# One-hot rows of a token's picks: four wide f16 operations with a step of four, or twelve narrow ones with per-partition scalars, side by side

## The chip, the cores and the metric

The kernel runs on 1 core of one Trainium2 chip. The metric is the device time of one execution in microseconds (us).

## The reference, cut to what matters

The program is two transformer blocks on 256 tokens of 1024 columns. The last part of the second block is a mixture of 16384 small experts ("PEER"): each of 8 heads picks 16 experts per token by two half keys, and the gates are a softmax over the 16 scores.

```python
best_s, pos = lax.top_k(cand_s, PEER_TOPK)
idx = jnp.take_along_axis(cand_i, pos, axis=-1)   # idx = i * 128 + j
g = jax.nn.softmax(best_s, axis=-1)
u = expert_u[idx]
act = jax.nn.gelu(jnp.einsum('cd,chkd->chk', xb, u).astype(jnp.float32), approximate=False)
w = (g * act).astype(xb.dtype)
return jnp.einsum('chk,chkd->cd', w, expert_v[idx])
```

A token has 8 x 16 = 128 picks, each a pair (i, j) with a gate g.

## The kernel before, in words

The kernel gathers no expert. It multiplies all 16384 rows of u with all tokens, in 128 blocks (i) of 128 rows (j), and weighs the result W[j, i, t] = gelu(u x) with a dense gate G[j, i, t] that is zero where token t did not pick (i, j). Then it multiplies W with all rows of v.

`peer` (L1261) holds this. Its main loop runs over 144 blocks of weights of 128x1024: 16 of the query weights, then 128 of u. For each block the program writes, in this order:

- `fetch` (L118), which loads a block three ahead by SP's queue, rounds it to float32r on ScalarE (`hi`, L114) and leaves the rest on VectorE (`lo`, L115); hi and lo have four buffers each;
- what is in the list `pend`: the spread of a group of gates into W, and the product of W with the gates that are known already (L1512);
- `proj_tile` (L352), 24 matmuls of 128x256 (L143 to L145) that need hi and lo of the block;
- what is in the list `late`: products of gates;
- gelu on ScalarE (L1508 into W for the tokens whose gates come later, L1511 into `act` for those whose gates are there);
- `work(PACE)` (L1429), which sets the order of the work around the change. VectorE's side work is a generator: the top-k of 8 heads, the lists of picks, then `gates` for eight tokens at a time, 32 times. Each piece yields the microseconds that it is booked at, and with every block pieces are taken until 1.4 of these are used up. VectorE's instructions stay in the order in which the program writes them.

`gates(n0)` (L1440) makes G for eight tokens. IT, JT, GH and GL hold, with the pick on the partition and the token on the column, the indices i and j and the gate in two f16 parts. For one token, G[j, i] = sum over the picks of onehot(j) onehot(i) g: a matmul over the 128 picks with bj (the one-hot of j) as weights and ah and al (the one-hot of i times the two parts) as moving operands. The rows of 128 are compared with `io4`, the numbers 0 to 127, each four times. Four operations on VectorE make them for eight tokens at once, with the four tokens of a group innermost, so that a token's row is read with a step of four elements:

```python
nc.vector.tensor_tensor(bj, hot, bc(JT), op=OP.is_equal)
nc.vector.tensor_tensor(ah, hot, bc(IT), op=OP.is_equal)
yield 1.2 * PGT
nc.vector.tensor_tensor(al, ah, bc(GL), op=OP.mult)
nc.vector.tensor_tensor(ah, ah, bc(GH), op=OP.mult)
```

`product` (L1455) issues eight matmuls for four tokens (L1459, L1460); `spread` (L1463) multiplies the result into W for the blocks that are done (VectorE, L1469) and copies it into W for those to come (ScalarE, L1471). ah, al and bj have two buffers each.

Of the kernel before, what the change touches and what calls it, by code (L numbers as in the profile page):

```python
# [12 lines left out]
F16 = mybir.dt.float16  # L13
# [4 lines left out]
OP = mybir.AluOpType  # L18
AX = mybir.AxisListType
DRAM = bass.MemoryType.DRAM  # L20
# [21 lines left out]
NTK, NLS, NGT = 11, 11, 3  # L42
# [33 lines left out]
class Body:  # L76
# [25 lines left out]
    # blocks of weights in the order of their use, each loaded and split exactly into two float32r parts  # L102
    def plan(self, *specs):
        """specs (name, index, width)"""
        self.todo.extend(specs)
# [12 lines left out]
    def fetch(self, n=None, low=None):  # L118
        """units loaded until the number ahead, or n more"""
        n = self.ahead - len(self.loaded) if n is None else n  # L120
        while self.todo and n > 0:
            spec = self.todo.popleft()
            self.loaded.append((spec[:2], self.load(*spec, low or (self.nc.gpsimd if spec[:2] in POOLED else self.nc.vector))))
            n -= 1
# [10 lines left out]
    def warm(self, n, p=None):  # L135
        """products of no use that keep TensorE's clock up through a wait"""
# [10 lines left out]
    def rstd(self, ss, n, width, beside=None):  # L147
        """1/sqrt(ss/width + eps) for ss [p, n]; beside: work in the wait for the square root"""
# [7 lines left out]
    def rstd_steps(self, ss, n, width):  # L156
        """the same as a list of steps"""
# [7 lines left out]
        # a step of Newton's on the table's value  # L165
# [9 lines left out]
    def setup(self):  # L175
# [3 lines left out]
        # the table of square roots, before its first use  # L179
# [3 lines left out]
        # rows of L1 columns, and 16 more behind the last  # L183
# [7 lines left out]
        # rows of tokens and the gate of the last sum; they wait in DRAM while the experts need their room  # L191
# [11 lines left out]
    # ---------------------------------------------------------------- the first block  # L203
    def ada_units(self, parts, acc, room):
        """silu(c) * w_ada of the parts named, summed over blocks of rows into acc; a block of 128 x 1024 each time"""
# [16 lines left out]
    def ada_cols(self, n0, s, later=None):  # L222
        """shift or scale s of the six (sh_a sc_a g_a sh_f sc_f g_f) as columns; later: takes what is left to be called"""
# [17 lines left out]
    def ada_row(self, s, dst, acc, ones, later=None):  # L241
        """gate s of the six on all partitions, from its sums acc"""
# [14 lines left out]
    def start(self, pool):  # L257
        """hn^T split; the meta rows between the two tiles of tokens"""
        nc, t = self.nc, self.t
        # in rooms that later tiles take  # L260
# [14 lines left out]
        def norm(tt):  # L275
            """1 / rms of a tile of rows, its halves squared beside each other"""
# [12 lines left out]
        def scaled(x, n, r, banks, w):  # L289
            """the transposes of x's rows, each times its r"""  # L290
# [49 lines left out]
    def proj(self, out, wh, wl, apart):  # L340
        """W^T x for a tile of columns; apart: the products with x's second part after the others"""
# [10 lines left out]
    def proj_tile(self, name, i=None, m=128, n=T, real=False):  # L352
        """W^T x for one tile of columns: bank [m, n] of the first n tokens, or without the meta rows between them"""
# [13 lines left out]
    def t5_bias(self, w):  # L367
        """per head [128 queries, keys]: keys of the block before, meta (for tile 1), of the block, meta (for tile 0)"""
# [13 lines left out]
        # a step back for each partition: from copies of the vectors, as many partitions at a time as there are copies  # L382
# [11 lines left out]
    # softmax of a pair of heads over two tiles of queries, then P V; the columns of a unit u = 2*tile + head  # L394
    def attend(self, outs, oc, qT, kT, bias, nk, sink, exp_scale, v, vmeta, gain, meta):
        """qT(tile, head), kT(head, n) give operands; bias(tile, head) an addend or None;
        nk the keys of each tile (the meta rows at 128, if meta); v(chunk, head) [128, 64]"""
# [7 lines left out]
        for tl in range(2):  # L405
            n, o = nk[tl], tl * nk[0]
            for hd in range(2):
                # the two heads' products run beside each other, each into its own bank
# [40 lines left out]
        # transposes of P: chunks of 128 keys  # L449
# [50 lines left out]
    def steps(self, gens, fills):  # L500
        """pairs of heads through the stages of attend, each stage a step after the one before; fills: work of TensorE
        beside them in each step"""
# [10 lines left out]
    def part(self, acc, items, tt, hf):  # L513
        """acc[tt][hf] += o[:, tt]^T w for items (o, w, start, stop)"""
# [4 lines left out]
    def out_proj(self, acc, items):  # L519
        """acc[tt][half] += o[:, tt]^T w for items (o, w, start, stop)"""  # L520
# [10 lines left out]
    def scaled_add(self, tt, hf, acc, r, row, add=None):  # L531
        """a half of h[:, tt] += acc * r * row"""
# [6 lines left out]
    def transposed4(self, src, hf):  # L539
        """bank with the transposes of four blocks of src's columns"""  # L540
# [8 lines left out]
    def pre(self, acc, t1, lnrow, ss, tt, hf, gain=True):  # L549
        """what the norm of acc takes from a finished half; gain: False for the squares alone, None for the gain alone"""  # L550
# [16 lines left out]
    def gained(self, p, y, c0, h, l, by, later=None):  # L567
        """a bank of transposes into operands, with gains from column c0 on; by: the engine of the second parts, which
        are put off into later"""
# [7 lines left out]
    def scaled(self, xn, r, tt, hf):  # L577
        """a half of h / rms(h), transposed"""
# [4 lines left out]
    def shifted(self, y, p, tt, hf, n0, by="act", steps=False):  # L583
        """a bank of transposes times 1 + scale and plus shift; or the steps of it"""
# [21 lines left out]
    def roots(self, x):  # L606
        """the table of square roots, once x is there"""
# [7 lines left out]
    def first_block(self):  # L615
# [21 lines left out]
        # forget gates: log sigmoid, then the sums over positions  # L637
# [6 lines left out]
        # c / (1 + exp(-c))  # L644
# [42 lines left out]
        def values(p, dst, c, dstm, zi):  # L687
            vT = A.tile([128, L1], F32, name=self.nm("vT"), tag="vT", bufs=2)
            nc.scalar.activation(vT, p, AF.Copy)
            # meta rows, one head to 16 partitions and its own columns  # L690
# [102 lines left out]
        # the last products and the step to the next operands; the gain goes on here, the rows' norm on the products  # L793
# [18 lines left out]
        with self.in_order(mybir.EngineType.PE):  # L812
# [10 lines left out]
            # the second tile's rows and what is added to them, transposed apart: the first of it needs no norm  # L823
# [919 lines left out]
```

## Time and profile before

| | |
|---|---|
| median of 3 runs | 1306.51 us (1304.98 to 1307.62) |
| profiled execution, span from the first to the last instruction | 1306.6 us |
| TensorE busy | 1269.4 us, 97% |
| VectorE busy | 970.5 us, 74% |
| ScalarE busy | 684.5 us, 52% |
| mean granted TensorE clock | 0.987 |

The profile shows one execution. It has no time of its own beside its span of 1306.6 us, which stands against the median of the runs. Engines are PE (TensorE's matmuls), PEld (its weight loads), DVE (VectorE), ACT (ScalarE), POOL (GpSimd) and SP (the queue of loads). A busy share is a mean over stages with different limits, so the stage is read from windows and from the timeline. Names such as `ps`, `lo` or `W` are the program's tiles.

### The profile page before, as it was taken

The numbers are of one execution on the slowest core, as the hardware profiler recorded it, in microseconds if no ns is written. First come the engines' busy times: TensorE is split into PE (matmuls) and PEld (weight loads), VectorE is DVE, ScalarE is ACT, GpSimd is POOL, SyncE is SP. The second block draws the span as 40 slices with busy tenths as digits, with TensorE's granted clock in tenths as the row PEclk, the third lists the DMA queues.
The fourth block names the chain that finished last, engine by engine and source line by source line (L and its number), as shares of the span: only waits on it lengthen the run. The fifth ranks groups of instructions, "written<-read, shape, count | busy, mean of one in ns | idle before, by whom it ended". The sixth has DMA issues, their size and how long they took to land.

```text
span 1306.6 us, 22860 instructions
## 1 busy us (share of the span) xinstructions
PE 1269.4 (97%) x8804; PEld 1160.8 (89%) x8804; DVE 970.5 (74%) x1908; ACT 684.5 (52%) x1241; POOL 86.8 (7%) x70
## 2 busy tenths in 40 slices
PE   8999999999888899999999999999999999999997
PEld 7887899999766699999999999999988888888886
DVE  5678878877777879989777889997555855555555
ACT  6655544454567455456555554445444554444543
POOL 2300100000351400000000000000000000000001
PEclk9999999999998989999999999999999999999999
DMA  6756588886241355555444444444576855555552
GB/s 216 217 188 216 184 289 292 285 281 226 62 135 31 116 191 169 186 169 192 158 135 146 146 145 145 139 149 167 186 253 208 296 195 186 193 177 193 190 185 93
DMA packets 67849, 239.50 MB, mean 183 GB/s; under 512 B 8499, under 2 KB 9155, under 8 KB 67452
## 3 DMA queue, kind: packets, MB, share of 16 engines
q1 hardware_dynamic: 66524, 233.53, 52.9%
q0 software_dynamic: 1216, 4.51, 1.1%
q8 instruction: 69, 1.13, 0.3%
q14 instruction: 40, 0.33, 0.1%
HBM read 235.87 MB, written 2.79 MB: 183 GB/s over the span
## 4 chain that ended last, share of the span: by engine, by line
PE 90%; DVE 7%; ACT 2%; DMA 1%; issue 1%; ACTq 0%; DVEq 0%
PE ps L143 24%; PE ps L144 23%; PE ps L145 23%; PE ps L345 3%; PE ps L348 3%; PE ps L347 3%; PE ps L1459 2%; PE ps L1460 2%; PE ps L410 1%; PE ps L465 1%; PE ps L480 1%; DVE lo L115 1%; PE ps L1486 1%; PE ps L229 0%; DVE h L537 0%
## 5 line engine op out<-in xcount | busy, mean ns | idle before, releaser
L114 ACT ACTIVATE hi<-x 128x1024 fp32r<-128x1024 f32 (+2 forms) x384 | 403.2, 1052 | 433.2 <-PE ps L145 181.6
L115 DVE TENSOR_TENSOR lo<-x,hi 128x1024 fp32r<-128x1024 f32 (+2 forms) x361 | 439.0, 1218 | 201.2 <-ACT hi L114 196.6
L143 PE MATMUL ps<-xh,hi 128*128 128x256 f32 (+2 forms) x1304 | 378.2, 290 | 1.4 <-ACT xh L573 1.0
L144 PE MATMUL ps<-xl,hi 128*128 128x256 f32 (+2 forms) x1304 | 368.5, 283 | 1.5 <-DVE xl L574 1.5
L145 PE MATMUL ps<-xh,lo 128*128 128x256 f32 (+2 forms) x1304 | 368.6, 283 | 0.0
L143 PEld LDWEIGHTS ps<-xh,hi 128*128 128x128 f32 (+1 forms) x1304 | 247.3, 190 | 3.2 <-ACT xh L573 1.2
L144 PEld LDWEIGHTS ps<-xl,hi 128*128 128x128 f32 (+1 forms) x1304 | 247.3, 190 | 2.7 <-POOL lo L115 1.7
L145 PEld LDWEIGHTS ps<-xh,lo 128*128 128x128 f32 (+1 forms) x1304 | 246.3, 189 | 0.6
L144 PE MATMUL ps<-lo,w 128*128 128x512 f32 (+1 forms) x640 | 223.3, 349 | 0.0
L143 PE MATMUL ps<-hi,w 128*128 128x512 f32 (+1 forms) x640 | 223.2, 349 | 0.0
L145 PE MATMUL ps<-hi,w 128*128 128x512 f32 (+1 forms) x640 | 221.9, 347 | 0.0
L143 PEld LDWEIGHTS ps<-hi,w 128*128 128x128 f32 x640 | 121.2, 189 | 16.9 <-ACT hi L114 0.2
L145 PEld LDWEIGHTS ps<-hi,w 128*128 128x128 f32 x640 | 120.8, 189 | 16.0
L144 PEld LDWEIGHTS ps<-lo,w 128*128 128x128 f32 x640 | 121.2, 189 | 15.4 <-issue 0.2
L345 PE MATMUL ps<-xh,hi 128*128 128x256 f32 x352 | 100.0, 285 | 0.6 <-ACT xh L573 0.6
L348 PE MATMUL ps<-xh,lo 128*128 128x256 f32 x352 | 98.7, 281 | 0.0
L347 PE MATMUL ps<-xl,hi 128*128 128x256 f32 x344 | 96.5, 281 | 0.0
L1469 DVE SCALAR_TENSOR_TENSOR W<-ps,W 128x160 f32<-128x160 f32 (+31 forms) x64 | 55.1, 865 | 31.0 <-ACT W L1508 30.2
L115 POOL TENSOR_TENSOR lo<-x,hi 128x1024 fp32r<-128x1024 f32 (+1 forms) x23 | 50.9, 2222 | 323.3 <-ACT hi L114 323.3
L345 PEld LDWEIGHTS ps<-xh,hi 128*128 128x128 f32 x352 | 66.2, 188 | 1.6 <-ACT xh L573 0.9
L348 PEld LDWEIGHTS ps<-xh,lo 128*128 128x128 f32 x352 | 66.3, 188 | 0.0
L347 PEld LDWEIGHTS ps<-xl,hi 128*128 128x128 f32 x344 | 65.1, 189 | 0.7
(346 smaller groups left out, 1706.2 us busy)
## 6 DMA issues: line engine op xcount, KB each, us to landing
x<-in_u SPq DMA_DIRECT2D x128, 512.0 KB, 3.5
x<-in_v SPq DMA_DIRECT2D x128, 512.0 KB, 3.5
x<-in_w_gu SPq DMA_DIRECT2D x44, 512.0 KB, 4.6
ada<-in_w_ada SPq DMA_DIRECT2D x40, 512.0 KB, 5.0
x<-in_w_down SPq DMA_DIRECT2D x22, 512.0 KB, 4.5
x<-in_w_in SPq DMA_DIRECT2D x18, 512.0 KB, 4.4
x<-in_w_out SPq DMA_DIRECT2D x16, 512.0 KB, 3.4
x<-in_w_query SPq DMA_DIRECT2D x16, 512.0 KB, 3.7
```

Source lines behind the costliest of these rows:

```text
L114: nc.scalar.activation(hi[:, :w], x[:, :w], AF.Copy)
L115: low.tensor_sub(lo[:, :w], x[:, :w], hi[:, :w].bitcast(F32))
L143: mm(out, lhsT=lh, rhs=rh, start=start, stop=False)
L144: mm(out, lhsT=lh, rhs=rl, start=False, stop=False)
L145: mm(out, lhsT=ll, rhs=rh, start=False, stop=stop)
L345: mm(out, lhsT=wh[:, s], rhs=self.xh[:, k, :T], start=k == 0, stop=False)
L347: mm(out, lhsT=wh[:, s], rhs=self.xl[:, k, :T], start=False, stop=False)
L348: mm(out, lhsT=wl[:, s], rhs=self.xh[:, k, :T], start=False, stop=not apart and k == KT - 1)
L410: nc.tensor.matmul(S[tl, hd], lhsT=qT(tl, hd), rhs=kT(hd, n), start=True, stop=True)
L1459: nc.tensor.matmul(o, lhsT=bj[:, gq, :, q], rhs=ah[:, gq, :, q], start=True, stop=False)
L1460: nc.tensor.matmul(o, lhsT=bj[:, gq, :, q], rhs=al[:, gq, :, q], start=False, stop=True)
L1469: nc.vector.scalar_tensor_tensor(a, pv[:, :, :i0], 1.0 / GSC, a, op0=OP.mult, op1=OP.mult)
```

## The change

The one-hot rows of a token now lie side by side: ah, al and bj are [128, 2, 4, 128] where they were [128, 2, 128, 4]. Each row is written by one tensor_scalar of 128 elements: `io` (the numbers 0 to 127, without repeats) is compared with a column of JT or IT that gives each partition its own number, and for ah and al multiplied in the same operation by a column of GH or GL. The matmuls read rows without a step. `io4` goes into a part of W that is scratch until the blocks fill it, is loaded after the sub keys and not ahead of them, and one copy in `lists` makes `io` from it. `gates` books 1.7 for each four tokens, in two pieces for eight tokens, where it booked 1.2, 1.2 and 0.8 in three (NGT is the number of pieces). The rest of the change takes out comments.

```diff
-NTK, NLS, NGT = 11, 11, 3
+NTK, NLS, NGT = 11, 11, 2
...
-        io4 = big.tile([128, 128, 4], F16, name="io4")
-        nc.sync.dma_start(io4, t["io4"])
+        io = big.tile([128, 128], F16, name="io")
...
+        io4 = carve((128, 4), F16)
+        nc.sync.dma_start(io4, t["io4"])
...
             nc.vector.tensor_copy(tif, tiu)
+            nc.vector.tensor_copy(io, io4[:, :, 0])
...
             ng = 2
-            sh = [128, ng, 128, NG4]
-
-            def bc(x):
-                return x[:, n0:n0 + ng * NG4].rearrange("p (g t) -> p g t", g=ng)[:, :, None, :].to_broadcast(sh)
-            hot = io4[:, None, :, :].to_broadcast(sh)
+            sh = [128, ng, NG4, 128]
             ah, al, bj = (pw.tile(sh, F16, name=self.nm(x), tag=x, bufs=2) for x in ("ah", "al", "bj"))
-            nc.vector.tensor_tensor(bj, hot, bc(JT), op=OP.is_equal)
-            nc.vector.tensor_tensor(ah, hot, bc(IT), op=OP.is_equal)
-            yield 1.2 * PGT
-            nc.vector.tensor_tensor(al, ah, bc(GL), op=OP.mult)
-            nc.vector.tensor_tensor(ah, ah, bc(GH), op=OP.mult)
+
+            def hots(gq):
+
+                for q in range(NG4):
+                    k = n0 + gq * NG4 + q
+                    key, hi, lo, j = (x[:, k:k + 1] for x in (IT, GH, GL, JT))
+                    nc.vector.tensor_scalar(bj[:, gq, q], io, j, None, op0=OP.is_equal)
+                    nc.vector.tensor_scalar(ah[:, gq, q], io, key, hi, op0=OP.is_equal, op1=OP.mult)
+                    nc.vector.tensor_scalar(al[:, gq, q], io, key, lo, op0=OP.is_equal, op1=OP.mult)
...
-                    nc.tensor.matmul(o, lhsT=bj[:, gq, :, q], rhs=ah[:, gq, :, q], start=True, stop=False)
-                    nc.tensor.matmul(o, lhsT=bj[:, gq, :, q], rhs=al[:, gq, :, q], start=False, stop=True)
+                    nc.tensor.matmul(o, lhsT=bj[:, gq, q], rhs=ah[:, gq, q], start=True, stop=False)
+                    nc.tensor.matmul(o, lhsT=bj[:, gq, q], rhs=al[:, gq, q], start=False, stop=True)
...
             for gq in range(ng):
+                hots(gq)
                 late.append(lambda gq=gq: product(gq))
-                yield (1.2 - 0.4 * gq) * PGT
+                yield 1.7 * PGT
...
-            x = pw.tile([128, 2, 128, NG4], F16, name=self.nm("w"), tag=("ah", "al", "bj")[i % 3], bufs=2)
+            x = pw.tile([128, 2, NG4, 128], F16, name=self.nm("w"), tag=("ah", "al", "bj")[i % 3], bufs=2)
```

How the instructions stand on VectorE's queue in the stage of the gates, before, for eight tokens (lo is the split of a block, ps the gate products, act the gelu):

```order
989 L1512 TENSOR_TENSOR W<-act_8430,W 128x80
990 L1449 TENSOR_TENSOR bj_8480<-io_5156,JT 128x1024
991 L1450 TENSOR_TENSOR ah_8478<-io_5156,IT 128x1024
992 L115 TENSOR_TENSOR lo_8485<-x_8483,hi_8484 128x1024
993 L1469 SCALAR_TENSOR_TENSOR W<-ps_8466,W 128x4x64
994 L1512 TENSOR_TENSOR W<-act_8476,W 128x84
995 L1452 TENSOR_TENSOR al_8479<-ah_8478,GL 128x1024
996 L1453 TENSOR_TENSOR ah_8478<-ah_8478,GH 128x1024
997 L115 TENSOR_TENSOR lo_8524<-x_8522,hi_8523 128x1024
```

Two operations stand ahead of each of two splits; the second pair reads what the first wrote. The same place of the changed kernel, one piece of four tokens between two splits:

```order
1259 L1515 TENSOR_TENSOR W<-act_8886,W 128x92
1260 L1453 TENSOR_SCALAR bj_8890<-io,JT 128x128
1261 L1454 TENSOR_SCALAR ah_8888<-io,IT,GH 128x128
1262 L1455 TENSOR_SCALAR al_8889<-io,IT,GL 128x128
1263 L1453 TENSOR_SCALAR bj_8890<-io,JT 128x128
1264 L1454 TENSOR_SCALAR ah_8888<-io,IT,GH 128x128
1265 L1455 TENSOR_SCALAR al_8889<-io,IT,GL 128x128
...
1271 L1455 TENSOR_SCALAR al_8889<-io,IT,GL 128x128
1272 L115 TENSOR_TENSOR lo_8963<-x_8961,hi_8962 128x1024
1273 L1471 SCALAR_TENSOR_TENSOR W<-ps_8937,W 128x4x69
```

Two wide operations stood ahead of a split, and eight tokens took four of them; now twelve narrow ones stand ahead of it for four tokens and twenty-four for eight.

On TensorE, a group of gate products and the block that follows it, in the changed kernel (ps of the 24 matmuls, then ps of the gates):

```order
4204 L145 MATMUL ps_7974<-xh,lo_7859 128x256
4205 L1461 LDWEIGHTS bj_7952
4206 L1461 MATMUL ps_7999<-ah_7950,bj_7952 128x128
4207 L1462 LDWEIGHTS bj_7952
4208 L1462 MATMUL ps_7999<-al_7951,bj_7952 128x128
...
4219 L1462 LDWEIGHTS bj_7952
4220 L1462 MATMUL ps_7999<-al_7951,bj_7952 128x128
4221 L143 MATMUL ps_8032<-xh,hi_7907 128x256
```

These rows stand where they stood, with the same numbers; L1459 and L1460 became L1461 and L1462, and the operands lost their step.

## Rows read from the trace of the kernel before

**Rows 1.** The page: the span, and busy time, share and instructions of two engines.
```profile
span 1306.6 us, 22860 instructions
...
PE 1269.4 (97%) x8804; PEld 1160.8 (89%) x8804; DVE 970.5 (74%) x1908; ACT 684.5 (52%) x1241; POOL 86.8 (7%) x70
```

**Rows 2.** Windows, the stage of the gates: busy us and instructions of each engine.
```profile
core 0: us, PE busy (x) PEld busy (x) DVE busy (x) ACT busy (x) POOL busy (x), PEclk, DMA share, GB/s
622.00:896.00 274.00, 274.00 (x2311) 270.51 (x2311) 233.87 (x340) 139.50 (x289) 0.00 (x0) 1.00 0.44 146
```

**Rows 3.** The chain that ended last, 622 to 900 us, shares by line.
```profile
by line: PE ps L143 26.2%; PE ps L144 25.9%; PE ps L145 25.9%; PE ps L1459 11.1%; PE ps L1460 10.8%; PE ps L1404 0.1%
```

**Rows 4.** Groups, 622 to 896 us: busy us, mean ns | idle before, and what ended it.
```profile
L115 DVE TENSOR_TENSOR lo<-x,hi 128x1024 fp32r<-128x1024 f32 x75 | 91.3, 1218 | 0.0
...
L1469 DVE SCALAR_TENSOR_TENSOR W<-ps,W 128x160 f32<-128x160 f32 (+31 forms) x64 | 55.1, 865 | 31.0 <-ACT W L1508 30.2 <-ACT act L1511 0.3
...
L1449 DVE TENSOR_TENSOR bj<-io,JT 128x1024 f16<-128x1024 f16 x32 | 21.9, 683 | 0.0
L1512 DVE TENSOR_TENSOR W<-act,W 128x4 f32<-128x4 f32 (+35 forms) x72 | 20.4, 283 | 6.8 <-ACT act L1511 6.8
```

**Rows 5.** Timeline of VectorE, 881 to 888 us: start us, us, instruction.
```profile
881.04 0.69 DVE L1449 TENSOR_TENSOR bj<-io,JT 128x1024 f16<-128x1024 f16 x1
...
882.24 1.23 DVE L115 TENSOR_TENSOR lo<-x,hi 128x1024 fp32r<-128x1024 f32 x1
883.38 1.17 DVE L1469 SCALAR_TENSOR_TENSOR W<-ps,W 128x436 f32<-128x436 f32 x1
...
884.79 0.68 DVE L1452 TENSOR_TENSOR al<-ah,GL 128x1024 f16<-128x1024 f16 x1
...
886.11 1.22 DVE L115 TENSOR_TENSOR lo<-x,hi 128x1024 fp32r<-128x1024 f32 x1
```

**Rows 6.** Timeline of VectorE at four other places: runs of four alike.
```profile
559.92 0.87 DVE L1327 MAX8 W<-W 128x8 f32<-128x128 f32 x4
...
582.59 0.90 DVE L1369 TENSOR_SCALAR W<-W 128x256 int32<-128x256 int32 x4
...
427.07 1.14 DVE L447 TENSOR_SCALAR sb<-sb,den 128x256 f32<-128x256 f32 x4
...
456.01 1.37 DVE L594 TENSOR_SCALAR ym<-ps,modT 128x128 f32<-128x128 f32 x4 [0.48 <-PE ps L543]
```

**Rows 7.** Groups of VectorE by shape, whole span: busy us, mean ns of one.
```profile
L1390 DVE TENSOR_TENSOR W<-W 128x2048 f16<-128x2048 f16 x4 | 4.7, 1218 | 0.0
...
L1327 DVE MAX8 W<-W 128x8 f32<-128x128 f32 x32 | 6.9, 281 | 0.0
...
L1369 DVE TENSOR_SCALAR W<-W 128x256 int32<-128x256 int32 x4 | 0.9, 290 | 0.0
...
L447 DVE TENSOR_SCALAR sb<-sb,den 128x256 f32<-128x256 f32 x24 | 7.0, 348 | 0.1
...
L594 DVE TENSOR_SCALAR ym<-ps,modT 128x128 f32<-128x128 f32 x16 | 5.6, 403 | 0.6 <-PE ps L543 0.5
...
L215 DVE TENSOR_SCALAR acc<-ada,csil 128x1024 f32<-128x1024 f32 x5 | 3.7, 746 | 1.0 <-DMA ada<-in_w_ada 0.9
```

**Rows 8.** Timeline of TensorE, 742 to 744 us: the first and last gate products.
```profile
742.52 0.29 PE L1459 MATMUL ps<-ah,bj 128*128 128x128 f16 x1
...
743.33 0.29 PE L1460 MATMUL ps<-al,bj 128*128 128x128 f16 x1
743.38 0.37 PE L143 MATMUL ps<-xh,hi 128*128 128x256 f32 x1
743.58 0.28 PE L144 MATMUL ps<-xl,hi 128*128 128x256 f32 x1
743.70 0.28 PE L145 MATMUL ps<-xh,lo 128*128 128x256 f32 x1
```

**Rows 9.** Timeline of TensorE at 476 us: the four products of the scores.
```profile
476.22 0.61 PE L1486 MATMUL ps<-W 128*128 128x128 f32 x4
```

## The prediction

> **What bounds the kernel now.** I read the page first, then the windows by stage, then the chain of waits, the groups of instructions and the timeline of the stage that the edit touches. The span is 1306.6 us and TensorE is busy for 97% of it, VectorE for 74% [rows 1]. The shares are means over stages, so the stage has to be looked at by itself. All gate work lies between 622 and 896 us, 274 us in which TensorE has no idle time and VectorE is busy for 233.9 us [rows 2]. VectorE's 40 us of idle time there are nearly all waits for ScalarE's gelu (31.0 us ahead of the spread of the gates at L1469, 6.8 us ahead of L1512) [rows 4]. The chain of this stretch agrees: every link is a matmul, and the two gate products hold 21.9% of its 278 us, 60.9 us, or 0.95 us for each of the 64 groups of eight [rows 3]. What is left, 274 - 60.9 = 213 us over the 75 blocks of weights that L115 splits there [rows 4], is 2.84 us a block. So TensorE sets the pace, and VectorE has 40 us to spare: 85% full. That slack is what the edit spends.
>
> **What the edit removes.** On VectorE, four operations of 128x1024 f16 for each eight tokens. A pair takes 1.20 us from start to start of what follows (881.04 to 882.24), the pair that multiplies 1.32 us (884.79 to 886.11) [rows 5]: 2.52 us, times 32 is 81 us. The rest of VectorE's work in the stage is therefore 233.9 - 81 = 153 us.
>
> **What it adds.** For each token three TENSOR_SCALARs of 128x128: bj with one column of per-partition scalars, ah and al with two. That is 12 in a piece of four tokens, 24 for eight, 768 in all. The trace has no f16 operation of this kind, so I build its price from four rows, always from start to start, since these operations overlap.
> - Fixed part: two f16 lengths of TENSOR_TENSOR, 2048 in 1.218 us [rows 7] and 1024 in 0.683 us [rows 4], give 0.522 ns an element; a pair at 0.60 us each [rows 5] then leaves 0.60 - 0.534 = 0.066 us.
> - Scalar column: four TENSOR_SCALARs of 256 elements without a column stand in 0.90 us, the mean of one being 0.290 us: (0.90 - 0.29)/3 = 0.203 us apart. With one column four take 1.14 us, the mean 0.348: 0.264 apart [rows 6, 7]. A column costs 0.061 us.
> - Two columns: four 128-element ones take 1.37 us, mean 0.403: 0.322 apart; MAX8 over 128 elements, without a column, is (0.87 - 0.281)/3 = 0.196 apart [rows 6, 7]. So two cost 0.126 us, and nothing of the second hides behind the first.
> - Elements: an f32 TENSOR_SCALAR goes at (746 - 348)/768 = 0.518 ns an element [rows 7]. On VectorE's two-operand operation f16 goes at half the f32 price: L115 takes 1.218 us for 1024 f32, L1449 0.683 us for as many f16 [rows 4]; less the 0.149 us that both carry this is 1.069 against 0.534. I take the same half here: 0.259 ns, 0.033 us for 128. The ends are 0 and the f32 pace, 0.066 us.
>
> So bj is 0.066 + 0.061 + 0.033 = 0.160 us and ah and al are 0.066 + 0.126 + 0.033 = 0.225 us each. A piece is 4 x 0.160 + 8 x 0.225 = 2.44 us, eight tokens 4.88 us, the whole 156 us in place of 81. The bounds: 134 us with elements free, 182 us at the f32 pace.
>
> A page has the price that the trace lacks. The Trainium skill, VectorE: DVE Perf Modes, section The perf-mode tier table, gives tensor_scalar on 16-bit data in SBUF four elements a cycle, which makes 0.033 us of 128 at its clock and the same sum. No run here shows it yet.
>
> **What moves.** The pacing counts 3.4 for eight tokens where it counted 3.2, against 1.4 a block, so eight tokens take 2.43 blocks and not 2.29. In the printed order 76 lo rows stand between the first and the last gate operation, where there were 71. These 5 blocks come from the stretch behind, which had no gate work, so they are only moved: 5 x 2.84 = 14 us join the stage, and VectorE gets 5 x (1.14 us of L115 and 0.3 us of L1512) = 7 us more there [rows 4, 5].
>
> **The sum.** For the same blocks TensorE needed 274 + 14 = 288 us. VectorE now needs 153 + 7 + 156 = 316 us. It no longer fits: VectorE, in order, becomes the bound, TensorE waits for lo (at most three blocks are prepared ahead), and the stage grows by 28 us less some 3 us by which VectorE may trail at its end while lo is ready ahead. What waits behind a piece is the next lo, the spread and with it ScalarE's L1471 and its next hi. The waits of VectorE of today (31.0 and 6.8 us) go, because TensorE and ScalarE are early now. 1306.6 + 25 = 1332 us, against a profiled execution of 1306.6 us that stands at the median of the runs, 1306.51. With the bounds: 134 us gives 294 needed, +6 us (1313); 182 us gives 342, +53 us (1360).
>
> Costed at nothing: the copy that makes io (one operation among the lists, where TensorE is never idle) and the load of io4, which goes behind two others on SP's queue and is first needed by the lists. TensorE's instructions keep their number and order. Whether the products get cheaper changes nothing while VectorE is the bound.
>
> **The rivals.**
> - *The f32 pace.* If a TENSOR_SCALAR on f16 gets nothing for being f16, 1360 us as above. For it: no row has the f16 form. Against it: the halving of the two-operand form.
> - *VectorE keeps up, the products cost what they did.* The stage stays TensorE's if a piece takes under (288 - 160)/64 = 2.0 us, that is 0.167 us an operation: if scalar columns cost less than half of what they do in f32. Then 1306.6 us. A rule stands behind this one: the same page, section The TRN2 errata, prices a VectorE operation at 58 cycles and the elements, with no term for a scalar column. By it a piece would take 1.13 us and the time would be 1306.6. The rows of L447 and L594 speak against it, at 0.061 and 0.126 us above their like without columns.
> - *VectorE keeps up and the products get cheaper: faster.* Eight products take 0.94 us (742.52 to 743.58, less one ordinary spacing of 0.12), 0.118 us each [rows 8], as much as a matmul with twice the columns. If the step of four elements is what holds them, a product without it could come down to half of that, 0.059 us: 64 x 8 x 0.059 = 30 us off, 1276 us. It needs a piece under (258 - 160)/64 = 1.53 us to come out whole; between 1.53 and 2.0 us it comes out in part, above 2.0 us it turns into a loss whatever TensorE gains. For it: the products' moving part is half as long as their neighbours'. Against it: the score products of 128 columns, which read without a step, are (0.61 - 0.274)/3 = 0.112 us apart [rows 9], and behind the last of the eight the next matmul starts 0.05 us later [rows 8], as if the load of weights and not the moving read filled the 0.118 us. A rule bears on it: the Trainium skill, TensorE: Matmul & The Clock Gate, section Weight-path perf modes, has the fast load of 16-bit weights on for 128 columns, packed or with a step. By that the step costs nothing, and this rival falls back to the one before it.
>
> **How the numbers follow.** The scalar columns decide between slower and the rest; both rows that show them agree within 3%, on f32. I give the forecast 0.50, with a range of its own of 1320 to 1342 (columns 10% cheaper or elements somewhat dearer). The f32 pace gets 0.15. That VectorE keeps up with products unchanged gets 0.12, with cheaper products 0.23, spread from 1276 to 1303, since no row shows an f16 column, and one may load cheaper than an f32 one. About 0.2% (2.6 us) is what a measurement can tell from no change. So slower 0.65, same 0.12, faster 0.23. The range of 1290 to 1360 leaves out about half of the faster case and the end of the f32 pace, some 0.17.
>
> **What the new profile would show.** Right: the three TENSOR_SCALAR groups x256 each, starts about 0.16 and 0.22 us apart, durations near 0.25 and 0.31 us; VectorE near full through the stage; TensorE's matmuls waiting for lo from L115; no more idle time ahead of L1471's spread on VectorE; the stage some 313 us long with 80 blocks. Wrong: TensorE without idle time in the stage, or starts under 0.167 us apart on the mean. A shorter spacing of the eight products would decide the third rival's half of the matter even if the time gets longer.

## The result and the profile after

The changed kernel takes 1328.95 us (median; 1327.52 to 1330.82) against 1306.43 us (1304.98 to 1307.62) for the kernel before on the same chip: 1.0167 times as long, with a 95% interval of 1.0148 to 1.0186. The prediction said 1332. The execution profiled after took 1327.52 us; its span, from the first to the last instruction, is 1325.7 us.

The page after, span and busy times:

```profile
span 1325.7 us, 23507 instructions
...
PE 1272.7 (96%) x8804; PEld 1142.5 (86%) x8804; DVE 1039.3 (78%) x2549; ACT 683.2 (52%) x1245; POOL 86.5 (7%) x70
```

VectorE has 641 instructions more than in [rows 1] (768 narrow ones and the copy for 128 wide ones) and TensorE as many as before. Means over the span still look like TensorE's kernel, 96%. The window over the stage of the gates does not:

```profile
622.00:920.00 298.00, 282.06 (x2340) 258.58 (x2339) 296.76 (x953) 139.75 (x292) 0.00 (x0) 1.00 0.41 133
```

In [rows 2] TensorE had no idle time and VectorE 40 us. Now VectorE is busy for 296.76 of 298 us and TensorE has 15.9 us without work. The chain of the stretch 622 to 935 us has changed engines with it; in [rows 3] every link was a matmul, now VectorE's lines hold 92%:

```profile
by line: DVE lo L115 26.2%; DVE al L1455 16.8%; DVE W L1471 15.7%; DVE bj L1453 15.2%; DVE ah L1454 13.8%; DVE W L1515 4.5%; issue 3.2%; PE ps L143 1.2%; PE ps L144 1.2%; PE ps L145 1.1%; ACT hi L114 0.3%; PE ps L1461 0.1%; DVE GL L1411 0.1
```

VectorE's timeline shows what fills it: a piece of four tokens between two splits. Its twelve operations stand at 0.16, 0.22 and 0.22 us, and the split that stood 1.20 or 1.32 us behind the first of two wide ones in [rows 5] comes 2.42 us behind the first of these:

```profile
760.62 0.43 DVE L1453 TENSOR_SCALAR bj<-io,JT 128x128 f16<-128x128 f16 x1
760.78 0.49 DVE L1454 TENSOR_SCALAR ah<-io,IT,GH 128x128 f16<-128x128 f16 x1
761.00 0.49 DVE L1455 TENSOR_SCALAR al<-io,IT,GL 128x128 f16<-128x128 f16 x1
761.22 0.43 DVE L1453 TENSOR_SCALAR bj<-io,JT 128x128 f16<-128x128 f16 x1
...
763.04 1.41 DVE L115 TENSOR_TENSOR lo<-x,hi 128x1024 fp32r<-128x1024 f32 x1
```

TensorE's timeline at one of the 17 groups, of 64, whose eight products still stand together: 0.057 us apart, where [rows 8] had 0.118, and the next matmul 0.43 us behind the first, where it came 0.86 us behind:

```profile
645.62 0.23 PE L1461 MATMUL ps<-ah,bj 128*128 128x128 f16 x1
645.68 0.22 PE L1462 MATMUL ps<-al,bj 128*128 128x128 f16 x1
...
646.02 0.22 PE L1462 MATMUL ps<-al,bj 128*128 128x128 f16 x1
646.05 0.36 PE L143 MATMUL ps<-xh,hi 128*128 128x256 f32 x1
```

If all 64 groups stood so, TensorE would be freed of 28 us (64 x 0.43). In this kernel they don't: 343 of the 512 products stand singly among the block's matmuls, as this one (L1462):

```profile
757.09 0.29 PE L144 MATMUL ps<-xl,hi 128*128 128x256 f32 x1
757.22 0.23 PE L1462 MATMUL ps<-al,bj 128*128 128x128 f16 x1
757.25 0.36 PE L145 MATMUL ps<-xh,lo 128*128 128x256 f32 x1
757.46 0.28 PE L143 MATMUL ps<-xh,hi 128*128 128x256 f32 x1
```

From 757.09 to 757.46 two matmuls and a product take 0.37 us, and two matmuls alone 0.24 (2 x 0.12), so the lone product costs 0.13 us; that is also the median of the 254 such places that have f32 matmuls on both sides. It is no less than the 0.118 us with the step. So as the products stand here, TensorE gained next to nothing. Why a lone product costs that much is open.

What TensorE waits for stands in the view of waits, TensorE and its weight loads, 622 to 920 us:

```profile
PE ps L1461 <- DVE ah L1454: 11.4, 24, 0.9
...
PEld L1461 <- DVE ah L1454: 13.4, 19, 1.1
PEld L1461 <- DVE bj L1453: 6.6, 14, 0.8
```

Where the time was lost is read from three places: the first gate operation, the last, and the first matmul with v. The timeline of before, then that of after:

```profile
622.15 0.68 DVE L1449 TENSOR_TENSOR bj<-io,JT 128x1024 f16<-128x1024 f16 x1
...
940.11 0.40 PE L143 MATMUL ps<-hi,w 128*128 128x512 f32 x1
```

```profile
619.54 0.25 DVE L1453 TENSOR_SCALAR bj<-io,JT 128x128 f16<-128x128 f16 x1
...
925.53 1.51 DVE L115 TENSOR_TENSOR lo<-x,hi 128x1024 fp32r<-128x1024 f32 x1
...
959.22 0.40 PE L143 MATMUL ps<-hi,w 128*128 128x512 f32 x1
```

| us | before | after | difference |
|---|---|---|---|
| first gate operation on VectorE | 622.15 | 619.54 | -2.6 |
| gate work, up to the split behind it (886.11, 925.53) | 264.0 | 306.0 | +42.0 |
| splits in between | 71 | 76 | 5 blocks, 14.2 at 2.84 |
| from there to the first matmul with v | 54.0 | 33.7 | -20.3 |
| first matmul with v | 940.11 | 959.22 | +19.1 |

The spans differ by the same 19.1 us (1325.7 less 1306.6), so all of it is lost ahead of the v stage. The medians differ by 22.5. In every run a time is 1.7 to 1.9 us above its span, so the profiled execution before would stand near 1308.4 us, above its median, and that of after is the fastest of its four.

### The profile page after: what moved, and what is told of

It is laid out like the page before. It is cut to its first block, busy times and chain, and to the rows that moved or that the text cites. A ratio compares the mean times of both kernels' runs of the same rounds, so it can differ in the third digit from the quotient of the medians.

```text
span 1325.7 us, 23507 instructions
## 1 busy us (share of the span) xinstructions
PE 1272.7 (96%) x8804; PEld 1142.5 (86%) x8804; DVE 1039.3 (78%) x2549; ACT 683.2 (52%) x1245; POOL 86.5 (7%) x70
## 3 DMA queue, kind: packets, MB, share of 16 engines
q8 instruction: 69, 1.13, 0.3%
## 4 chain that ended last, share of the span: by engine, by line
PE 66%; DVE 28%; ACT 2%; issue 2%; DMA 1%; DVEq 0%; ACTq 0%
PE ps L143 18%; PE ps L144 17%; PE ps L145 17%; DVE lo L115 7%; DVE al L1455 4%; DVE W L1471 4%; DVE bj L1453 4%; DVE ah L1454 3%; PE ps L345 3%; PE ps L348 3%; PE ps L347 3%; PE ps L410 1%; DVE W L1515 1%; DMA x<-in_w_down 1%; PE ps L465 1%
## 5 line engine op out<-in xcount | busy, mean ns | idle before, releaser
L115 DVE TENSOR_TENSOR lo<-x,hi 128x1024 fp32r<-128x1024 f32 (+2 forms) x361 | 454.2, 1260 | 199.1 <-ACT hi L114 197.8
L143 PE MATMUL ps<-xh,hi 128*128 128x256 f32 (+2 forms) x1304 | 386.6, 297 | 1.4 <-ACT xh L573 1.0
L144 PE MATMUL ps<-xl,hi 128*128 128x256 f32 (+2 forms) x1304 | 375.1, 288 | 2.0 <-DVE xl L574 1.5
L145 PE MATMUL ps<-xh,lo 128*128 128x256 f32 (+2 forms) x1304 | 375.0, 288 | 0.0
L1455 DVE TENSOR_SCALAR al<-io,IT,GL 128x128 f16<-128x128 f16 x256 | 123.3, 482 | 0.0
L1454 DVE TENSOR_SCALAR ah<-io,IT,GH 128x128 f16<-128x128 f16 x256 | 123.0, 481 | 0.0
L1453 DVE TENSOR_SCALAR bj<-io,JT 128x128 f16<-128x128 f16 x256 | 107.4, 420 | 0.0
L115 POOL TENSOR_TENSOR lo<-x,hi 128x1024 fp32r<-128x1024 f32 (+1 forms) x23 | 50.6, 2208 | 322.9 <-ACT hi L114 322.8
L1461 PE MATMUL ps<-ah,bj 128*128 128x128 f16 x256 | 53.2, 226 | 16.8 <-DVE ah L1454 12.4
```

What stands on the lines that cost most here:

```text
L115: low.tensor_sub(lo[:, :w], x[:, :w], hi[:, :w].bitcast(F32))
L143: mm(out, lhsT=lh, rhs=rh, start=start, stop=False)
L144: mm(out, lhsT=lh, rhs=rl, start=False, stop=False)
L145: mm(out, lhsT=ll, rhs=rh, start=False, stop=stop)
L1453: nc.vector.tensor_scalar(bj[:, gq, q], io, j, None, op0=OP.is_equal)
L1454: nc.vector.tensor_scalar(ah[:, gq, q], io, key, hi, op0=OP.is_equal, op1=OP.mult)
```

## Experiments

The theory after the result: (a) the narrow operations fill VectorE, and it is their scalar columns that make them too dear; (b) products without the step are cheaper for TensorE, which the time of the kernel after does not show. The rivals: the loss comes from TensorE, where the products of after stand singly among the block's matmuls for the most part; or the shorter spacing of the products is something else than the step. Ratios are to the kernel before, with 95% intervals.

### Who sets the time: the step taken out, and put in again

The kernel before, its wide operations kept, with products that read 128 elements side by side:

```diff
-                    nc.tensor.matmul(o, lhsT=bj[:, gq, :, q], rhs=ah[:, gq, :, q], start=True, stop=False)
...
+                fb, fh, fl = (x[:, gq].rearrange("p a b -> p (a b)") for x in (bj, ah, al))
...
+                    r = slice(q * 128, (q + 1) * 128)
+                    nc.tensor.matmul(o, lhsT=fb[:, r], rhs=fh[:, r], start=True, stop=False)
...
```

> The kernel before, VectorE's four wide operations kept, but the gate products read 128 elements side by side (the gates are mixed up among tokens). Theory: the step of four costs TensorE 0.118 - 0.057 us a product, 0.43 us for each of 64 groups, 28 us; VectorE's 234 us still fit into 274 - 28 = 246 us. Time 1279 to 1288 us, starts of the eight 0.057 us apart. Rival, the load of weights sets the 0.118 us and the step costs nothing: 1306 us, starts 0.118 us apart.

Measured: 1280.51 us (1277.51 to 1281.58), ratio 0.9791 [0.9767, 0.9814]. TensorE's timeline, the eight products of a group, and the window:

```profile
743.87 0.23 PE L1461 MATMUL ps<-ah,bj 128*128 128x128 f16 x1
...
744.27 0.22 PE L1462 MATMUL ps<-al,bj 128*128 128x128 f16 x1
744.30 0.36 PE L143 MATMUL ps<-xh,hi 128*128 128x256 f32 x1
```

```profile
622.00:880.00 258.00, 257.55 (x2408) 254.65 (x2407) 239.50 (x353) 142.25 (x302) 0.00 (x0) 1.00 0.50 162
```

With VectorE's operations as they were, TensorE keeps the pace (257.55 of 258 us) and the shorter products come out whole: 26 us, against 28 worked out from the timeline. So a product without the step is worth this to TensorE where all groups stand together, as they do here (runs of eight and sixteen).

The reverse, in the kernel after: its narrow operations, and products that read with a step of four again:

```diff
-                    nc.tensor.matmul(o, lhsT=bj[:, gq, q], rhs=ah[:, gq, q], start=True, stop=False)
...
+                fb, fh, fl = (x[:, gq].rearrange("p a b -> p (a b)").rearrange("p (a b) -> p a b", b=4) for x in (bj, ah, al))
...
+                    nc.tensor.matmul(o, lhsT=fb[:, :, q], rhs=fh[:, :, q], start=True, stop=False)
...
```

> The changed kernel, VectorE's narrow operations kept, but the products read with a step of four again (the gates are mixed up). Theory: VectorE's 316 us are the bound of the stage and TensorE needs 288 us with the step, so the time stays that of the changed kernel, 1327 to 1333 us. Rival, TensorE's side (products in between the blocks' matmuls, waiting for the rows) holds the longer time: 64 x 0.43 = 28 us more, 1355 us.

Measured: 1331.93 us (1330.11 to 1333.12), ratio 1.0192 [1.0169, 1.0215], 3 us from the kernel after, with overlapping intervals. Window, and the group of the first products:

```profile
622.00:920.00 298.00, 280.99 (x2312) 271.06 (x2311) 295.54 (x943) 142.52 (x290) 0.00 (x0) 1.00 0.42 133
```

```profile
L1462 PE MATMUL ps<-ah,bj 128*128 128x128 f16 x248 | 64.2, 295 | 17.0 <-DVE ah L1454 15.5 <-ACT act L1515 1.0 <-ACT W L1512 0.3
```

The products are as long as before (295 ns), VectorE is as full (295.54 us), and the time hardly moves. This kernel answers the rival of the single products: in its printed order they stand in runs of eight (24) or of seven and one (40), and the time is the same. It does not show that a dearer TensorE is hidden, because TensorE's load hardly rises: with the step a product in such a run takes 0.119 us, and the lone ones of the kernel after took 0.13.

### The price of the scalar columns

The kernel after with constants in place of the columns; first all of them, then those of the gates alone:

```diff
-                    nc.vector.tensor_scalar(bj[:, gq, q], io, j, None, op0=OP.is_equal)
-                    nc.vector.tensor_scalar(ah[:, gq, q], io, key, hi, op0=OP.is_equal, op1=OP.mult)
...
+                    nc.vector.tensor_scalar(bj[:, gq, q], io, 5.0, None, op0=OP.is_equal)
+                    nc.vector.tensor_scalar(ah[:, gq, q], io, 5.0, 2.0, op0=OP.is_equal, op1=OP.mult)
...
```

> The changed kernel with constants in place of every column of per-partition scalars (the gates are then the same for all picks); number, shape and order of operations are the same. Theory: an operation costs 0.066 + 0.033 = 0.099 us, a piece 1.19 us, VectorE needs 153 + 7 + 76 = 236 us and falls below TensorE's 260 us: 1279 to 1285 us. Rival, it is the number of operations that makes the stage VectorE's and columns are nearly free: 1325 us or more.

Measured: 1278.41 us (1276.89 to 1279.73), ratio 0.9781 [0.976, 0.9802]. VectorE's timeline of a piece, and the chain of 622 to 900 us:

```profile
740.04 0.17 DVE L1453 TENSOR_SCALAR bj<-io 128x128 f16<-128x128 f16 x1
740.14 0.17 DVE L1454 TENSOR_SCALAR ah<-io 128x128 f16<-128x128 f16 x1
740.24 0.17 DVE L1455 TENSOR_SCALAR al<-io 128x128 f16<-128x128 f16 x1
...
741.26 1.21 DVE L115 TENSOR_TENSOR lo<-x,hi 128x1024 fp32r<-128x1024 f32 x1
```

```profile
by line: PE ps L143 30.8%; PE ps L144 29.3%; PE ps L145 29.2%; PE ps L1461 5.5%; PE ps L1462 5.1%; PE ps L1406 0.1%
```

Twelve operations take 1.22 us, 0.102 each, and the chain is TensorE's again. As many instructions as in the kernel after, and 50 us less: their number is not the trouble. One thing changed beside the columns: in its printed order all products stand in runs of eight, so TensorE's gain is in these 50 us too. The next kernel has the same order, and one column in each operation:

```diff
-                    nc.vector.tensor_scalar(ah[:, gq, q], io, key, hi, op0=OP.is_equal, op1=OP.mult)
...
+                    nc.vector.tensor_scalar(ah[:, gq, q], io, key, 2.0, op0=OP.is_equal, op1=OP.mult)
...
```

> The changed kernel with a constant in place of the gate columns GH and GL alone: every operation has one column (the gates are then left out). Theory: 0.160 us each, a piece 1.92 us, VectorE 153 + 7 + 123 = 283 us against TensorE's 260: still the bound, 1306 + 283 - 288 - 3 = 1298 us. Rival, a second column hides behind the first and nothing is saved: 1329 us; rival, columns matter only from two on: 1279 us.

Measured: 1305.06 us (1302.64 to 1308.13), ratio 0.9993 [0.9977, 1.001]. The piece of VectorE's timeline:

```profile
741.54 0.25 DVE L1453 TENSOR_SCALAR bj<-io,JT 128x128 f16<-128x128 f16 x1
741.70 0.25 DVE L1454 TENSOR_SCALAR ah<-io,IT 128x128 f16<-128x128 f16 x1
...
743.49 1.22 DVE L115 TENSOR_TENSOR lo<-x,hi 128x1024 fp32r<-128x1024 f32 x1
```

1.95 us, 0.163 each: the second column of ah and al costs (2.42 - 1.95)/8 = 0.059 us and the first (1.95 - 1.22)/12 = 0.061. No column, one, two: 1278, 1305, 1329 us. The first step, 27 us, is the columns' alone, since order and number are the same on both sides; with the second the order changed too. The 7 us above the 1298 that was expected are a miss. The piece came as priced, but the sum took VectorE as the bound throughout, and here it is not quite full:

```profile
622.00:880.00 258.00, 253.46 (x2212) 239.37 (x2210) 251.97 (x906) 124.64 (x277) 0.00 (x0) 1.00 0.46 146
```

It is busy for 251.97 of 258 us, where the kernel after had 296.76 of 298. Whether these 6 us are the whole of the miss is not shown.

### Which operand's step costs

Only bj narrow and side by side (it is the weights), ah and al wide, read with the step (they are the moving operands):

```diff
-            nc.vector.tensor_tensor(bj, hot, bc(JT), op=OP.is_equal)
...
+            bj = pw.tile([128, ng, NG4, 128], F16, name=self.nm("bj"), tag="bj", bufs=2)
...
+            def hots(gq):
+                for q in range(NG4):
+                    k = n0 + gq * NG4 + q
+                    nc.vector.tensor_scalar(bj[:, gq, q], io, JT[:, k:k + 1], None, op0=OP.is_equal)
...
-                    nc.tensor.matmul(o, lhsT=bj[:, gq, :, q], rhs=ah[:, gq, :, q], start=True, stop=False)
...
+                    nc.tensor.matmul(o, lhsT=bj[:, gq, q], rhs=ah[:, gq, :, q], start=True, stop=False)
...
```

> bj alone side by side by narrow operations with one column (8 x 0.160 = 1.28 us for eight tokens), ah and al by the wide ones with the step (1.92 us): VectorE needs 153 + 102 = 255 us. If the step of the weights is what made a product dear, the products fall to 0.057 us, TensorE needs 246 us, VectorE is just the bound: 1285 to 1292 us. If the step of the moving operand is: products stay 0.118 us apart, TensorE needs 274 us: 1306 us.

Measured: 1304.64 us (1302.6 to 1307.43), ratio 0.9989 [0.9977, 1.0002]. TensorE's timeline, the products 0.117 us apart:

```profile
742.19 0.30 PE L1468 MATMUL ps<-al,bj 128*128 128x128 f16 x1
742.31 0.29 PE L1467 MATMUL ps<-ah,bj 128*128 128x128 f16 x1
...
742.89 0.29 PE L1468 MATMUL ps<-al,bj 128*128 128x128 f16 x1
```

Weights side by side change next to nothing. The 32 x (8 x 0.16 - 0.60) = 22 us more on VectorE fit into its 40 us. The other way round, ah and al narrow with both columns as in the kernel after, and bj wide, read with the step as weights (lines against the kernel after):

```diff
-                    nc.vector.tensor_scalar(bj[:, gq, q], io, j, None, op0=OP.is_equal)
...
+            nc.vector.tensor_tensor(bj, hot, bc(JT), op=OP.is_equal)
...
-                    nc.tensor.matmul(o, lhsT=bj[:, gq, q], rhs=ah[:, gq, q], start=True, stop=False)
...
+                    nc.tensor.matmul(o, lhsT=bj[:, gq, :, q], rhs=ah[:, gq, q], start=True, stop=False)
...
```

> ah and al side by side by narrow operations with two columns (3.60 us for eight tokens), bj by the wide one with the step (0.60 us), read as weights: VectorE needs 153 + 7 + 134 = 294 us. Theory: the weights' step is free, so the eight stand 0.057 us apart where they are ready, but VectorE is the bound: 1306 + 294 - 288 - 3 = 1309 us. Rival, weights with a step load in 0.118 us: spacing 0.118 us, time 1309 us as well.

Measured: 1309.78 us (1306.0 to 1312.92), ratio 1.0025 [1.0009, 1.0041]. The products:

```profile
703.75 0.22 PE L1466 MATMUL ps<-al,bj 128*128 128x128 f16 x1
...
704.09 0.22 PE L1466 MATMUL ps<-al,bj 128*128 128x128 f16 x1
```

0.057 us apart, with the weights' step in place. The step of the moving operand costs; that of the weights is nearly free (a load of weights takes 0.114 to 0.118 us on the mean where it took 0.097 without it, and the products keep their distance). ah and al are the dear ones to write narrow, which is why the time is no better than before.

### A version that uses this

G[j, i] may be summed with the gate on either side. So the one-hot of i, without a gate and hence with one column, becomes the narrow, moving operand (the tile that was bj), and the one-hot of j times the gate's parts stays wide and stepped, as weights:

```diff
+                    nc.vector.tensor_scalar(bj[:, gq, q], io, IT[:, k:k + 1], None, op0=OP.is_equal)
...
-            nc.vector.tensor_tensor(ah, hot, bc(IT), op=OP.is_equal)
...
+            nc.vector.tensor_tensor(ah, hot, bc(JT), op=OP.is_equal)
...
-                    nc.tensor.matmul(o, lhsT=bj[:, gq, :, q], rhs=ah[:, gq, :, q], start=True, stop=False)
-                    nc.tensor.matmul(o, lhsT=bj[:, gq, :, q], rhs=al[:, gq, :, q], start=False, stop=True)
+                    nc.tensor.matmul(o, lhsT=ah[:, gq, :, q], rhs=bj[:, gq, q], start=True, stop=False)
+                    nc.tensor.matmul(o, lhsT=al[:, gq, :, q], rhs=bj[:, gq, q], start=False, stop=True)
```

> The moving operand is the one-hot of i without gates, side by side, by narrow operations with one column (1.28 us for eight tokens); the weights are the one-hot of j times the two gate parts, by the wide operations, read with the step (1.92 us). Theory: only the moving operand's step costs, so the eight stand 0.057 us apart and TensorE needs 246 us; VectorE needs 153 + 102 = 255 us: 1279 to 1288 us, faster than both kernels. Rival, a step in either operand costs the full 0.118 us: 1306 us.

Measured: 1287.49 us (1286.51 to 1291.61), ratio 0.9864 [0.9841, 0.9886]: faster than both kernels. Products and window:

```profile
700.72 0.22 PE L1468 MATMUL ps<-bj,al 128*128 128x128 f16 x1
...
701.05 0.22 PE L1468 MATMUL ps<-bj,al 128*128 128x128 f16 x1
```

```profile
622.00:880.00 258.00, 250.82 (x2325) 246.37 (x2324) 251.19 (x563) 134.32 (x296) 0.00 (x0) 1.00 0.48 153
```

Eight tokens cost VectorE 8 x 0.16 + 1.92 = 3.20 us here (2.52 before, 2 x 2.42 = 4.84 after), and the products stand 0.055 us apart though each loads other weights than the one before it. Both engines have some 7 us to spare in the window now. Three attempts on what is left to the 1280.5 of the first experiment. First, some of u's splits given to GpSimd:

```diff
-POOLED = [("w_out_2", c) for c in (0, 1, 2, 3, 4, 5, 6, 7)] + [("w_swa", c) for c in (0, 1, 2, 4, 5, 6, 7)] + [("w_kvup", None), ("w_qup", 0), ("w_qup", 1)]
+POOLED = [("w_out_2", c) for c in (0, 1, 2, 3, 4, 5, 6, 7)] + [("w_swa", c) for c in (0, 1, 2, 4, 5, 6, 7)] + [("w_kvup", None), ("w_qup", 0), ("w_qup", 1)] + [("u", i) for i in range(40, 116, 4)]
```

> The kernel with swapped operands, and lo of 19 blocks of u (every fourth of those in the stage) on GpSimd at 2.2 us each: VectorE needs 255 - 19 x 1.14 = 233 us, below TensorE's 246. Theory: if VectorE still holds the swapped kernel, this gives back up to 9 us, 1277 to 1280 us; if TensorE already sets the pace there, no change. Rival: GpSimd's lo comes late or slows VectorE, slower than the swapped kernel.

Measured: 1298.73 us (1295.07 to 1303.12), ratio 0.9944 [0.9922, 0.9966], 11 us slower than without it. VectorE's timeline, four narrow operations alone and four while GpSimd splits; then GpSimd's split itself:

```profile
707.04 0.74 DVE L1456 TENSOR_SCALAR bj<-cols,IT 128x128 f16<-128x128 f16 x4
707.69 1.22 DVE L115 TENSOR_TENSOR lo<-x,hi 128x1024 fp32r<-128x1024 f32 x1
...
708.99 2.89 DVE L1456 TENSOR_SCALAR bj<-cols,IT 128x128 f16<-128x128 f16 x4
```

```profile
707.67 3.67 POOL L115 TENSOR_TENSOR lo<-x,hi 128x1024 fp32r<-128x1024 f32 x1 [9.84 <-ACT hi L114]
```

The four take 2.89 us instead of 0.74, most of it beside GpSimd's 3.67; VectorE's own split beside it keeps its 1.22 us. But narrow f16 operations are not the only ones that are held. Beside the next of GpSimd's splits (721.90 to 725.20 us) it is the f32 multiplication of the gelu into W (L1522), and beside a later one (837.98 to 840.49) VectorE's split itself:

```profile
723.54 1.77 DVE L1522 TENSOR_TENSOR W<-act,W 128x100 f32<-128x100 f32 x1
...
838.16 3.41 DVE L115 TENSOR_TENSOR lo<-x,hi 128x1024 fp32r<-128x1024 f32 x1
```

The multiplication of 128x100 takes 0.26 us in the kernel without GpSimd's splits. Beside each of the 19 splits exactly one operation of VectorE is held: 13 times L1522, five times a narrow one, once L115. The first two kinds end within 0.25 us of the split's end, L115 1.08 us behind it. Against the same operations in the kernel without the edit they are 1.2 to 2.2 us longer, 33 us in all, and the splits taken off VectorE save 19 x 1.14 = 22 us; the difference of 11 us is about what the time lost. GpSimd's splits took 2.40 to 4.17 us, where 2.2 were expected.

Second, the gate work booked at 1.15 times its cost, so that it spreads over more blocks; third, the same at 1.1 in the kernel after:

```diff
-PTK, PLS, PGT = 1.0, 1.0, 1.0
+PTK, PLS, PGT = 1.0, 1.0, 1.15
```

> The kernel with swapped operands, its gate pieces booked 15% dearer, so that they spread over 84 blocks in place of 73 and VectorE's free time behind the stage is used. VectorE needs 153 + 11 x 1.44 + 102 = 271 us for these blocks, TensorE 84 x 2.84 + 64 x 0.51 = 271 us. Theory, VectorE was the bound in the first 73: 1279 to 1283 us, against 1287 us. Rival, what holds the swapped kernel is TensorE or ScalarE: no change, 1287 us.

Measured: 1286.48 us (1283.64 to 1287.18), ratio 0.9833 [0.9809, 0.9857], not to be told from the version without it (the intervals overlap), though TensorE waits half as long: the group of its first products, without the edit and with it:

```profile
L1467 PE MATMUL ps<-bj,ah 128*128 128x128 f16 x256 | 36.8, 226 | 7.2 <-DVE ah L1461 5.4 <-ACT act L1521 1.7
```

```profile
L1467 PE MATMUL ps<-bj,ah 128*128 128x128 f16 x256 | 37.2, 226 | 3.3 <-DVE ah L1461 3.1
```

> The changed kernel, its pieces booked 10% dearer: 85 blocks in place of 78. VectorE needs 153 + 12.4 x 1.44 + 156 = 327 us, where TensorE took 274 + 12.4 x 2.84 = 309 us before: 18 us more in place of the 28 us worked out for the changed kernel, so about 10 us less than it, 1319 us. Rival, the booking is only an order and VectorE's work is done at the same time: 1329 us.

Measured: 1324.55 us (1321.05 to 1327.56), ratio 1.0123 [1.0089, 1.0157]: 4.4 us less than the kernel after, where 10 were expected. The intervals of the two overlap here too, so that spreading helps where VectorE is the bound is likely but not shown. What keeps the swapped version 7 us above the first experiment is for the most part TensorE's wait ahead of the first product, as far as single executions tell: the spans of the first experiment, of the spread version and of the swapped one are 1279.4, 1281.9 and 1284.7 us, and that wait is 0.5, 3.3 and 7.2 us.

## Why the prediction was right

**The price of the narrow operations** was right to 1%: 2.44 us a piece predicted, 2.42 measured, 64 x 2.42 = 155 us against 156. Its parts hold too: the f32 rows' columns, 0.061 and 0.126 us, against 0.061 and 0.120 on f16; fixed part and elements, 0.099 us without a column against 0.102. So the f32 pace, 0.033 us more, is out; how the 0.102 us divide into fixed part and elements no run shows. Some of this was luck: the 0.126 us came from a row that reads ps, set against a MAX8, another kind of operation. One bound was added up wrongly: with the elements free the whole is 156 - 768 x 0.033 = 131 us, not 134, which makes the lower end +3 us (1310) and not +6 (1313).

**The rule without columns.** The Trainium skill, VectorE: DVE Perf Modes, section The TRN2 errata, prices a VectorE operation by a fixed term and its elements. By that estimate 1.13 us a piece; the kernel without columns took 1.22, so the trace agrees within 8% where no column is read, and the kernel after, at 2.42, shows that the columns come on top. The rival that rested on it had its condition right as well: with the columns free, VectorE keeps up.

**VectorE as the bound**: right. 296.76 of 298 us, the waits ahead of the spread and of L1515 gone, as said: the only wait left on VectorE in that window is 1.2 us ahead of GL (L1411). The five blocks that move into the stage are there (71 splits, now 76).

**The sum.** Gate work grew by 42.0 us, 14.2 of them the moved blocks: 27.8 left, where the prediction had 28. What VectorE may trail by was put at 3 us; the table above shows 2.6 us by an earlier start and 20.3 - 14.2 = 6.1 us less behind the stage, 8.7 in all. The earlier start had no term in the sum, and the trailing was put at half of its 6.1 us; together they are the reason why the span grew by 19.1 us and not by 25. The trailing shows in the splits: taken in order, a block's lo was ready 7.4 us ahead of its first use in the kernel before and 2.0 us in the kernel after (medians, 800 to 890 us).

**What TensorE waits for**: wrong. The prediction named lo from L115, and the waits are for the one-hot rows ah and bj, 31.4 us in the three lines of the waits view (weight loads and matmuls overlap, so they don't add up to idle time). Splits are prepared up to three blocks ahead and were never late: through the stage lo was ready at least 0.9 us before its first use, while the rows of a group are written just before its products are due. On the time it made no difference, since both stand in the same queue of a full engine.

**"TensorE's instructions keep their number and order"**: the number yes, the order no. In the printed order of after the products stand mostly singly among the block's matmuls (343 of the 512), before in runs of eight (56) and sixteen (4). The eight products in a row that are shown ahead of the prediction as standing where they stood are one of 17 such groups. The experiment with the step put in again shows that this did not set the time.

**The third rival's doubt**: wrong. The prediction held against cheaper products that score products without a step are 0.112 us apart [rows 9] and that the load of weights fills 0.118 us. The score products have f32 operands, these f16, and products of f16 come at 0.057 us once the moving operand lies side by side. The Trainium skill, TensorE: Matmul & The Clock Gate, section Weight-path perf modes, has the fast load of weights for a read that is packed or strided, and the kernel with only the weights stepped agrees (0.057 us). It was an error to stretch this to the moving operand, of which the section does not speak. The rival's own price, 0.059 us and 30 us in all, was right, and 26 us came out where VectorE was left alone. It fell by its condition, a piece under 1.53 us, which the columns break; in the kernel after the products also stand singly for the most part, which the rival did not foresee.

## What to carry to other kernels

Cutting one wide operation into many narrow ones is to be priced from start to start and by its per-partition columns (here 0.06 us each, on 0.10 us without one), and held against the slack of that engine in that stage. Where a layout serves a matmul, ask which of its operands gains, and whether the products still follow each other: here only the moving one did, and only in runs, so it was enough to write the cheapest of the three tiles side by side and to make that one move. A gain on one engine is only seen by leaving the other alone, as the first experiment did.

## What was not expected of the hardware

- A step of four f16 elements in the moving operand doubles a product of 128 columns in a run of eight, 0.118 against 0.057 us; the same step in the weights costs next to nothing, even where every product loads other weights (0.055 us). A lone f16 product among f32 matmuls costs 0.13 us without any step.
- Beside each of 19 splits on GpSimd one operation of VectorE was held until about the split's end, and took 1.2 to 2.2 us longer than without it. It was a narrow f16 one, an f32 multiplication or once a split, while others beside the same splits kept their time. What picks the one that is held is open.
- In the profile after, the durations on VectorE's rows drift upward through the stage while the starts keep their distance. The timeline at its end:

```profile
924.93 0.54 DVE L1453 TENSOR_SCALAR bj<-io,JT 128x128 f16<-128x128 f16 x1
925.09 0.60 DVE L1454 TENSOR_SCALAR ah<-io,IT,GH 128x128 f16<-128x128 f16 x1
```

bj takes 0.25 us at 619.54, 0.43 at 760.62 and 0.54 here, and stands 0.16 us ahead of the next each time. L115 drifts with it, 1.22 us at 618.40 and 1.51 at 925.53, and is back at 1.22 at 944.72. Sums of such durations say little, distances of starts do. The cause is open.
